# Half of a decoder layer's output product by seven products in the first layer too, its steps dealt out among the other parts

## The chip, the cores and the metric

The kernel runs on one core of one Trainium2 chip. The metric is the time of one execution in device microseconds (us); three runs of the kernel before give 1916.87 us as their median (1916.32 to 1916.96). Engines are named as the profile names them: PE (matmuls), PEld (PE's weight loads), DVE, ACT, POOL, SP.

## The reference

Two decoder layers on 256 tokens (two tiles of 128) of width 2048. Cut to what matters here:

```
for l in range(DEPTH):
    h = rms_norm(x, norm1_g[l])
    z = h @ w_in[l]
    z_sgu = gelu(z[..., :2048])
    out_a = chunked_sgu(z_sgu, sgu_norm_g[l], sgu_w[l], sgu_b[l])
    out_b = swa_sink_attention(q, k, v, ...)          # the other columns of z
    mixed = concatenate([rms_norm(out_a, out_norm_a[l]), rms_norm(out_b, out_norm_b[l])])
    x = x + mixed @ w_out[l]
    h2 = rms_norm(x, norm2_g[l])
    x = x + (silu(h2 @ w_gate[l]) * (h2 @ w_up[l])) @ w_down[l]
```

The place of the change is `mixed @ w_out[l]` for the first layer: a 256 x 2048 by 2048 x 2048 product. The first 1024 rows of `w_out` meet `out_a` (the gated half, "a"), the other 1024 meet `out_b` (attention, "b"). The two normalisations are applied behind the product, as a factor for each token.

## The kernel before, in words

**One unit of product.** Weights come as tiles `raw` of 128 x 1024 (512 KB) over SP's queue into eight buffers. `split2` makes two parts of each in a reduced form of float32: ACT writes `wh` (L118, five buffers), DVE subtracts and writes `wl` (L119, four buffers). `mm3` then runs three matmuls of 128 x 512 for each of 128 rows and each token tile: wh with the high part of the activation (L154), wl with the high part (L155), wh with the low part (L156). A `unit` is 12 such matmuls into two accumulators, one for each token tile.

**Order.** Nothing runs by itself: the program is written as a stream of units, `tick()` adds one to a clock for each unit (a half for a half unit), and small steps (attention, normalisation, transposes) are booked with `later(delay, step)` and put into the program when the clock is due. The tables at the head (`UNIT_AT`, `END_AT`, `PARTS`) are such bookings, a first entry for the first layer and a second for the second. The build then sets the final order on each engine, so that a row may stand some rows from where the program has it.

**The stage.** Behind the q, k, v and gate products stands the product of the two u blocks (`u_gated`), and then the output product in parts: `a0` is column block 0 (512 columns) from the a half, `b2` is column block 2 from the b half. Each part is four units; `PARTS` is their order, one name for a unit. In between come six attention units (`attend`, each with scores `ps_s` L617, a softmax on DVE and ACT, transposes of the probabilities `ps_p` L654 and the product with the values `ps_v` L666), booked by `UNIT_AT`. Four `attend_end` steps, booked by `END_AT`, transpose attention's output `ob` (L227, `ps_t`) and make the activations of the b parts with L217 on ACT and L218 on DVE. `to_T` in `u_gated` transposes the gated u into `aT` for the a parts.

**Banks.** Matmul results go to eight banks: five of the pool `pa` (accumulators), two of `pd`, one of `pm`. `small_ps` hands the small tiles (`ps_s`, `ps_p`, `ps_v`, `ps_t`) round four homes: `pm`, `pd`, `pd`, `pa`. While `few` is set the fourth is left out.

**The second layer already does it the other way.** There `S_OUT` is true: column blocks 2 and 3 of the a half are one product of 2 x 2 blocks by `seven_low`, in 14 half units of six matmuls, each an entry `s` of `PARTS`, in place of eight units. `seven_low` needs the activations also in summed form: `combine_a` makes, beside the usual pair, four sums (L279, L282, L285 on DVE) and splits them into `ext` (L291 on ACT, L292 on DVE). The weights are summed on DVE (L433, L434), and two more sums are made by transfers of POOL's queue that add to what lies in the buffer (`ys` L435, `ss` L440). The products are held in three accumulators `l0`, `l1`, `l2` of `pa`.

Of the kernel before, what the change touches and what calls it, by code (L numbers as in the profile page):

```python
# [46 lines left out]
STD_UNITS = 8 * NFF + 16 * len(GU_BLOCKS)  # L47
TAIL = 16
WARM = 12
UNIT_AT = ((8, 11, 14, 17, 20, 24), (8, 11, 14, 17, 21, 25))  # L50
KV_NORM = (31, 0)
KV_T = (8, 6)
V_NORM = ((12, 2), (0, 0))
# [7 lines left out]
Q_T = (((4, 6), (6, 9)), ((4, 6), (4, 7)))  # L61
SPATIAL_AT = (((8, 10), (9, 11)), ((6, 9), (7, 10)))
U_AT = (((5, 8), (2, 4)), ((3, 7), (2, 3)))
END_AT = (((22, 26), (30, 32)), ((22, 27), (31, 33)))
S_OUT = (False, True)
EXT_A_WAIT = 0.5
FF_FIRST = 5
EXT_AT = (6.5, 8, 11, 13, 16, 18, 21.5, 24)
MASK_AFTER = ((5, 5), (4, 4))
GATE_LOAD = ((24, 29), (5, 15))  # L70
PARTS = (
    "a0 a0 a1 a1 a0 a0 a1 a1 a2 a2 a2 a2 a3 a3 a3 a3 b0 b0 b1 b1 b0 b0 b1 b1 b2 b2 b2 b2 b3 b3 b3 b3",
    "a0 a0 s a0 s a0 a1 a1 s a1 s a1 s b0 s b0 s b0 s b0 s b1 s b1 s b1 s b1 s s b2 b2 b2 b2 b3 b3 b3 b3",
)

# [12 lines left out]
def trunk(ctx, tc, x, xt, w_in, w_q, w_out, w_oa, w_gate, w_up, w_down, sgu_w, sgu_g, consts,  # L88
# [39 lines left out]
    def later(delay, fn):  # L128
        pending.append((clock[0] + delay, next(serial), fn))
# [71 lines left out]
    def small(shape, name):  # L201
        return sp.tile(shape, F32, tag=name, name=name)
# [20 lines left out]
    def transpose_pair(blocks, ps=None):  # L223
        ps = small_ps([P, 2, SEQ], "ps_t") if ps is None else ps
        for j in range(2):
            for t in range(NTOK):
                nc.tensor.transpose(  # L227
                    ps[:, j, t * P : (t + 1) * P], blocks[t][:, j * P : (j + 1) * P], ident
                )
        return ps  # L230
# [5 lines left out]
    def finish_rms(ss, width):  # L236
        tot = small([P, NTOK], "tot")
        nc.vector.tensor_reduce(tot, ss, AX.X, ALU.add)
        r = inv_rms(tot, NTOK, width)
        return [r[:, t : t + 1] for t in range(NTOK)]  # L240
# [64 lines left out]
    def combine_a(ps, lay, col, ext):  # L305
        ge = tp.tile([P, 2, NB], F32, tag="hT", name="ge")
        g = ge[:, 0].rearrange("p (j c) -> p j c", j=2)
        for j in range(2):
            nc.scalar.activation(
                g[:, j, :], ps[:, j, :], AF.Copy, scale=cst[:, lay, col + j : col + j + 1]  # L310
            )
        pair = tp.tile([P, 2, 2, SEQ], F32R, tag="aT", name="aT")
        nc.scalar.copy(pair[:, 0], g)
        nc.vector.tensor_tensor(pair[:, 1], g, f(pair[:, 0]), ALU.subtract)
        extend(g, tp, "hT", ext, EXT_A_WAIT, ge[:, 1].rearrange("p (n c) -> p n c", n=4))
        return pair
# [194 lines left out]
    for lay in range(L):  # L511
# [169 lines left out]
        def attend_end(gp, r, lay=lay, ob=ob, ssb=ssb, pairs_b=pairs_b):  # L681
            if r == 0:
                for t in range(NTOK):
                    sum_sq(ssb[:, t, gp : gp + 1], ob[gp, t])
            g = 2 * gp + r
            ps = transpose_pair([ob[gp, t][:, r * 2 * P : (r + 1) * 2 * P] for t in range(NTOK)])
            pairs_b[g] = split_gain(ps, lay, C_GB + 2 * g, "aT")
# [61 lines left out]
        def u_gated(b, acc, lay=lay, layer=layer, gate=gate, ssa=ssa, pairs_a=pairs_a, ext_a=ext_a):  # L749
# [17 lines left out]
            def to_T(c):  # L767
                ps = transpose_pair([us[t][:, 2 * c * P : (2 * c + 2) * P] for t in range(NTOK)])
                if S_OUT[lay]:
                    pairs_a.append(combine_a(ps, lay, C_GA + 4 * b + 2 * c, ext_a))  # L770
# [50 lines left out]
        for i, (gp, t, i0, n) in enumerate(units):  # L821
            at = UNIT_AT[lay][i]
            later(at, lambda gp=gp, t=t, i0=i0, n=n, attend=attend: attend(gp, t, i0, n))
# [3 lines left out]
        for gp in range(2):  # L827
            for r in range(2):
                later(END_AT[lay][gp][r], lambda gp=gp, r=r, attend_end=attend_end: attend_end(gp, r))
        rstds = {}  # L830

        def finish_mixed(kind, ss, lay=lay, rstds=rstds):
            rstds[kind] = finish_rms(ss, SW)
            if kind == "a" and S_OUT[lay]:
                na = small([P, NTOK], "na")

                def negate():
                    for t in range(NTOK):
                        nc.vector.tensor_scalar(
                            na[:, t : t + 1], rstds["a"][t], -1.0, None, ALU.mult  # L840
                        )

                later(3, negate)
                rstds["na"] = [na[:, t : t + 1] for t in range(NTOK)]

        later(END_AT[lay][1][0] + 1, lambda ssb=ssb, finish_mixed=finish_mixed: finish_mixed("b", ssb))
        if lay > 0:
# [342 lines left out]
```

## Time and profile before

| | |
|---|---|
| median of three runs | 1916.87 us (1916.32 to 1916.96) |
| the profiled execution's own time | 1915.77 us |
| its span | 1914.0 us |
| instructions | 25417 |
| moved by transfers | 456.84 MB, mean 239 GB/s |

The profile is of one execution, and durations are read from it. Its span is 1.77 us shorter than that execution's own time, which holds what lies around the span. Matmuls overlap in the records: one of 128 x 512 is shown with 0.39 us, while the next starts some 0.23 us behind it; what counts is the distance between starts.

### The profile page before, as it was taken

How to read it: one execution, taken by the hardware profiler on the slowest of the kernel's cores; microseconds unless marked ns; L12 is line 12 of the kernel's file. 1: busy time of each engine (PE TensorE's matmuls, PEld its weight loads, DVE VectorE, ACT ScalarE, POOL GpSimd, SP SyncE). 2: the span in 40 equal slices, each digit the busy share in tenths (PEclk: the TensorE clock that was granted, in tenths of full speed). 3: DMA queues.
4: the chain of work that ended last, by engine and by line, in shares of the span. 5: the costliest groups of instructions: out<-in, count | busy, mean ns of one | idle time of the engine just before them, and what ended most of it. 6: DMA issues, size and time to landing. Idle time of an engine off the chain costs nothing.

```text
span 1914.0 us, 25417 instructions
## 1 busy us (share of the span) xinstructions
PE 1907.2 (100%) x8776; PEld 1569.2 (82%) x8776; DVE 1709.5 (89%) x1853; ACT 1353.1 (71%) x1814; POOL 182.5 (10%) x176
## 2 busy tenths in 40 slices
PE   9999999999999999999999999999999999999999
PEld 7888888888888888888888888888888888888887
DVE  7987689999999999999796778899999999999993
ACT  8668577677767776777777577766877677766774
POOL 0231001000100001000012201000000100010000
PEclk9999999999999999999999999999999999999999
DMA  9974448888877897888577537697789778888783
GB/s 355 262 284 154 135 160 239 255 247 276 267 237 245 271 292 226 249 255 288 187 216 263 182 120 232 191 271 231 242 269 295 229 247 266 277 243 252 251 273 112
DMA packets 127425, 456.84 MB, mean 239 GB/s; under 512 B 14144, under 2 KB 14528, under 8 KB 127296
## 3 DMA queue, kind: packets, MB, share of 16 engines
q1 hardware_dynamic: 105264, 376.44, 53.5%
q0 software_dynamic: 21312, 77.60, 22.2%
q8 instruction: 68, 1.11, 0.2%
q10 hardware_dynamic: 720, 1.18, 0.2%
q14 instruction: 61, 0.50, 0.1%
HBM read 453.07 MB, written 2.10 MB: 238 GB/s over the span
## 4 chain that ended last, share of the span: by engine, by line
PE 97%; issue 1%; DVE 1%; ACT 0%; POOL 0%; DMA 0%; SPq 0%; DVEq 0%; ACTq 0%; POOLq 0%
PE m L155 15%; PE m L154 15%; PE m L156 15%; PE dacc L154 11%; PE dacc L155 11%; PE dacc L156 11%; PE acc L154 5%; PE acc L155 5%; PE acc L156 5%; PE ps_v L666 1%; PE ps_f L227 1%; PE ps_s L617 1%; PE ps_n L227 1%; PE ps_p L654 0%; PE ps_t L227 0%
## 5 line engine op out<-in xcount | busy, mean ns | idle before, releaser
L118 ACT CAST wh<-raw 128x1024 fp32r<-128x1024 f32 (+1 forms) x794 | 815.3, 1050 | 396.6 <-DVE raw L350 168.7
L119 DVE TENSOR_TENSOR wl<-raw,wh 128x1024 fp32r<-128x1024 f32 (+1 forms) x794 | 944.7, 1217 | 99.2 <-ACT wh L118 25.9
L154 PE MATMUL m<-wh,ext 128*128 128x512 f32 x704 | 276.7, 393 | 0.0
L155 PE MATMUL m<-wl,ext 128*128 128x512 f32 x704 | 274.9, 391 | 0.0
L156 PE MATMUL m<-wh,ext 128*128 128x512 f32 x704 | 274.4, 390 | 0.0
L155 PE MATMUL dacc<-wl,aT 128*128 128x512 f32 x624 | 243.4, 390 | 0.0
L154 PE MATMUL dacc<-wh,aT 128*128 128x512 f32 x624 | 243.2, 391 | 0.0
L156 PE MATMUL dacc<-wh,aT 128*128 128x512 f32 x624 | 243.0, 389 | 0.0
L119 DVE TENSOR_TENSOR wl<-t,wh 128x1024 fp32r<-128x1024 f32 x176 | 213.0, 1219 | 12.7 <-issue 5.2
L118 ACT CAST wh<-t 128x1024 fp32r<-128x1024 f32 x176 | 184.5, 1051 | 37.6 <-DVE t L351 14.1
L154 PE MATMUL m<-wh,hT 128*128 128x512 f32 x528 | 206.4, 391 | 0.0
L155 PE MATMUL m<-wl,hT 128*128 128x512 f32 x528 | 205.7, 390 | 0.0
L156 PE MATMUL m<-wh,hT 128*128 128x512 f32 x528 | 205.5, 389 | 0.0
L155 PEld LDWEIGHTS m<-wl,ext 128*128 128x128 f32 x704 | 132.3, 188 | 29.0 <-DVE wl L119 2.1
L154 PEld LDWEIGHTS m<-wh,ext 128*128 128x128 f32 x704 | 132.2, 188 | 27.5 <-ACT wh L118 0.8
L156 PEld LDWEIGHTS m<-wh,ext 128*128 128x128 f32 x704 | 132.1, 188 | 27.5
L154 PEld LDWEIGHTS dacc<-wh,aT 128*128 128x128 f32 x624 | 117.2, 188 | 25.2 <-ACT wh L118 0.8
L155 PEld LDWEIGHTS dacc<-wl,aT 128*128 128x128 f32 x624 | 117.2, 188 | 24.8 <-DVE wl L119 0.6
L156 PEld LDWEIGHTS dacc<-wh,aT 128*128 128x128 f32 x624 | 117.2, 188 | 24.3
L154 PE MATMUL acc<-wh,aT 128*128 128x512 f32 x304 | 121.8, 402 | 0.0
L359 POOL DMA_DIRECT2D t<-in_w_gate_dram x80 | 69.3, 866 | 524.7 <-DVE wl L119 393.1
L156 PE MATMUL acc<-wh,aT 128*128 128x512 f32 x304 | 119.1, 392 | 0.0
(190 smaller groups left out, 2841.9 us busy)
## 6 DMA issues: line engine op xcount, KB each, us to landing
raw<-in_w_gate_dram SPq DMA_DIRECT2D x176, 512.0 KB, 5.9
raw<-in_w_up_dram SPq DMA_DIRECT2D x176, 512.0 KB, 6.0
raw<-in_w_down_dram SPq DMA_DIRECT2D x176, 512.0 KB, 5.9
t<-in_w_gate_dram POOLq DMA_DIRECT2D x80, 512.0 KB, 7.6
raw<-in_w_in_dram SPq DMA_DIRECT2D x76, 512.0 KB, 5.6
raw<-in_w_out_dram SPq DMA_DIRECT2D x56, 512.0 KB, 3.4
raw<-in_w_up_dram POOLq DMA_DIRECT2D x40, 512.0 KB, 6.1
raw<-in_w_q_dram SPq DMA_DIRECT2D x32, 512.0 KB, 5.2
```

The lines of the kernel that those rows point to most:

```text
L118: nc.scalar.copy(wh[:, j : j + step, :], src)
L119: nc.vector.tensor_tensor(wl[:, j : j + step, :], src, f(wh[:, j : j + step, :]), ALU.subtract)
L154: nc.tensor.matmul(acc, ah, wh, start=first, stop=False, skip_group_check=again)
L155: nc.tensor.matmul(acc, ah, wl, start=False, stop=False, skip_group_check=again)
L156: nc.tensor.matmul(acc, al, wh, start=False, stop=last, skip_group_check=again)
L227: nc.tensor.transpose(ps[:, j, t * P : (t + 1) * P], blocks[t][:, j * P : (j + 1) * P], ident)
L359: anchor[0] = nc.gpsimd.dma_start(t2, src(1, 0, i), accum_op=ALU.add)
L617: nc.tensor.matmul(ps[r][:, i, :], qT[gp][rows, i0 + i, t * P : (t + 1) * P], kT[rows, gp, :nk], start=True, stop=True,)
L666: nc.tensor.matmul(pv[:, r, i], pt[:, (r * n + i) * (t + 1) + b, :], zkv[b][:, cols], start=b == 0, stop=b == t,)
```

## The change

Three tables of the first layer change. `S_OUT` becomes true for it, so that parts a2 and a3 (eight units) go and 14 half units `s` come. `PARTS` deals these out among a0, a1, b0 and b1, so the b parts begin five units of the clock sooner. `UNIT_AT` and `END_AT` move the attention steps of the first layer forward by half a tick to five ticks.

```
-UNIT_AT = ((8, 11, 14, 17, 20, 24), (8, 11, 14, 17, 21, 25))
+UNIT_AT = ((7.5, 10, 12.5, 15.5, 18, 20.5), (8, 11, 14, 17, 21, 25))
...
-END_AT = (((22, 26), (30, 32)), ((22, 27), (31, 33)))
-S_OUT = (False, True)
+END_AT = (((21, 23.5), (25.9, 27)), ((22, 27), (31, 33)))
+S_OUT = (True, True)
...
 PARTS = (
-    "a0 a0 a1 a1 a0 a0 a1 a1 a2 a2 a2 a2 a3 a3 a3 a3 b0 b0 b1 b1 b0 b0 b1 b1 b2 b2 b2 b2 b3 b3 b3 b3",
+    "a0 a0 a1 a1 s a0 a0 s a1 s a1 s s s b0 s b0 s b0 s b0 s b1 s b1 s b1 s b1 s b2 b2 b2 b2 b3 b3 b3 b3",
```

In the final order of each engine the two programs are the same up to the second u block and again from block b2 on, tile numbers apart. PE has 96 matmuls of 128 x 512 fewer for a2 and a3, and 84 for the 14 half units: 12 fewer. The stretches of small tiles between such matmuls number 23 where they were 25. DVE gets 6 splits more (L119), 4 sums of weights (L433, L434), 4 times L279, L282, L285, L292 and L314 in place of 8 times L218, and 2 of L865 fewer at each accumulator for 4 of L872 and 2 sums of results. ACT has two loads of its function table fewer.

On PE, at the first place, the scores of the fourth attention unit (`ps_s`) stand ahead of two groups of transposes. Before, all matmuls of one bank come first and then those of the other, and a unit of part a0 follows:

```order
L654 MATMUL ps_p_1814<-ident_103,s_1682 128x128 x4
L654 MATMUL ps_p_1820<-ident_103,s_1682 128x128 x4
L617 MATMUL ps_s0_1827<-kT_123,qT1_125 128x128 x4
L617 MATMUL ps_s1_1828<-kT_123,qT1_125 128x128 x4
L154 MATMUL acc0_1616<-wh_1849,aT_1790 128x512
```

Now they alternate between the two banks, and the transposes of the last gated u (`ps_t_1841`) follow a matmul later:

```order
L617 MATMUL ps_s0_1808<-kT_123,qT1_125 128x128
L617 MATMUL ps_s1_1809<-kT_123,qT1_125 128x128
L617 MATMUL ps_s0_1808<-kT_123,qT1_125 128x128
L617 MATMUL ps_s1_1809<-kT_123,qT1_125 128x128
L654 MATMUL ps_p_1829<-ident_103,s_1647 128x128 x4
L654 MATMUL ps_p_1835<-ident_103,s_1647 128x128 x4
L154 MATMUL acc0_1627<-wh_1878,aT_1729 128x512
L227 MATMUL ps_t_1841<-ident_103,u_1622 128x128
L227 MATMUL ps_t_1841<-ident_103,u_1624 128x128
```

What moved: the scores have the next transposes close behind, where they had a whole unit of 12. Four accumulators (a0 and a1) are open here, so `ps_s0_1808` has the fifth bank of `pa`, and `ps_t_1841` is booked on the same one.

On PE, at the second place, the first `attend_end` (`ps_t` from `ob`) and the transposes of the next probabilities. Before:

```order
L227 MATMUL ps_t_2003<-ident_103,ob_1783 128x128
L666 MATMUL ps_v_2015<-zkv_340,pt_1924 128x64 x8
L154 MATMUL acc0_1956<-wh_2028,aT_1712 128x512
L155 MATMUL acc0_1956<-wl_2029,aT_1712 128x512
L156 MATMUL acc0_1956<-wh_2028,aT_1712 128x512
```

behind which stand nine matmuls more of the same unit, and then `ps_p`. Now:

```order
L227 MATMUL ps_t_2065<-ident_103,ob_1780 128x128
L666 MATMUL ps_v_2077<-zkv_340,pt_1974 128x64 x8
L654 MATMUL ps_p_2089<-ident_103,s_1921 128x128 x4
L154 MATMUL l1_2013<-wh_2108,ext_1760 128x512
L155 MATMUL l1_2013<-wl_2109,ext_1760 128x512
L156 MATMUL l1_2013<-wh_2108,ext_1760 128x512
L154 MATMUL l1_2013<-wh_2108,ext_1873 128x512
L654 MATMUL ps_p_2095<-ident_103,s_1921 128x128 x4
L155 MATMUL l1_2013<-wl_2109,ext_1873 128x512
```

What moved: between `ps_t_2065` and `ps_p_2095`, which take the same bank of `pd` one after the other, there are four large matmuls. Three homes are in turn here, four before.

On DVE, at the same place, the drains of that bank are the two L218 on `aT_2070`. Before, the rows around them (`aT_2008`) are:

```order
L119 TENSOR_TENSOR wl_2099<-raw_2096,wh_2098 128x1024
L659 TENSOR_TENSOR rden_1950<-den_1949,es_1948 128x4
L660 RECIPROCAL rden_1950<-rden_1950 128x4
L119 TENSOR_TENSOR wl_2135<-raw_2132,wh_2134 128x1024
L218 SCALAR_TENSOR_TENSOR aT_2008<-ps_t_2003,cst_82,aT_2008 128x256
L673 TENSOR_TENSOR ob_2024<-ps_v_2015,rden_1843 128x512
L218 SCALAR_TENSOR_TENSOR aT_2008<-ps_t_2003,cst_82,aT_2008 128x256
```

Now:

```order
L119 TENSOR_TENSOR wl_2123<-ys_1858,wh_2122 128x1024
L622 SCALAR_TENSOR_TENSOR s_2025<-ps_s0_2026,bias_1664 128x512
L622 SCALAR_TENSOR_TENSOR s_2025<-ps_s1_2027,bias_1666 128x512
L119 TENSOR_TENSOR wl_2133<-ys_1959,wh_2132 128x1024
L631 TENSOR_REDUCE m_2034<-s_2025 128x4
L218 SCALAR_TENSOR_TENSOR aT_2070<-ps_t_2065,cst_82,aT_2070 128x256
L632 SCALAR_TENSOR_TENSOR nm_2035<-m_2034,nsink_608 128x4
L673 TENSOR_TENSOR ob_2086<-ps_v_2077,rden_1824 128x512
L633 TENSOR_TENSOR es_2036<-nm_2035,nsink_608 128x4
L865 SCALAR_TENSOR_TENSOR xres_108<-acc0_1740,ir2_1786,xres_108 128x512
L218 SCALAR_TENSOR_TENSOR aT_2070<-ps_t_2065,cst_82,aT_2070 128x256
```

What moved: the scores and the maximum of the sixth attention unit, a split of a summed weight `ys` and an update of the residual now stand ahead of the second drain.

## Prediction

> **What bounds the kernel now.** I read the page first: busy times, then the chain of work that ended last.
>
> ```profile
> PE 1907.2 (100%) x8776; PEld 1569.2 (82%) x8776; DVE 1709.5 (89%) x1853; ACT 1353.1 (71%) x1814; POOL 182.5 (10%) x176
> PE 97%; issue 1%; DVE 1%; ACT 0%; POOL 0%; DMA 0%; SPq 0%; DVEq 0%; ACTq 0%; POOLq 0%
> ```
>
> PE is the bound from end to end, and the chain is PE's own order. So a matmul taken away is time won, one for one, and whatever else the change does costs nothing until PE has to wait for it. Whether PE waits today at the place of the change is read from the windows of the first layer's attention and output stage (start and end, length, then busy us and instructions of PE, PEld, DVE, ACT, POOL, the clock, the DMA share, GB/s), and from two of the second layer, where the same product already runs by halves.
>
> ```profile
> 160.00:180.00 20.00, 19.95 (x118) 16.25 (x117) 13.77 (x25) 19.55 (x42) 0.89 (x1) 1.00 0.30 100
> 180.00:200.00 20.00, 20.00 (x119) 17.27 (x118) 14.47 (x25) 15.39 (x42) 0.73 (x1) 1.00 0.48 159
> 200.00:220.00 20.00, 20.00 (x112) 16.23 (x111) 14.64 (x22) 10.00 (x20) 0.00 (x0) 1.00 0.42 137
> sum 160.00, PE 159.94 PEld 133.02 DVE 117.88 ACT 110.91 POOL 8.78; mean PE 19.99 PEld 16.63 DVE 14.74 ACT 13.86 POOL 1.10
> 1140.00:1160.00 20.00, 20.00 (x115) 17.14 (x114) 17.54 (x34) 15.73 (x34) 2.50 (x3) 1.00 0.54 161
> 1160.00:1180.00 20.00, 20.00 (x92) 16.21 (x91) 17.14 (x21) 13.09 (x18) 3.17 (x3) 1.00 0.88 224
> ```
>
> PE does not wait (159.94 of 160 us from 140 to 300 us); the clock is full, and DVE has a quarter of the time free (117.88 of 160). The second layer runs its halves without a wait of PE, with DVE at 17.5 of 20; but there all six attention units are through, or nearly so, when the halves begin. In the first layer the two now fall together, with ACT at 19.55 of 20 in one window already. That decides the case.
>
> **What PE has less of.** The distance between starts, from the timeline of PE:
>
> ```profile
> 163.11 0.39 PE L155 MATMUL acc<-wl,hT 128*128 128x512 f32 x1
> ...
> 165.41 0.39 PE L156 MATMUL acc<-wh,hT 128*128 128x512 f32 x1
> 165.65 0.60 PE L227 MATMUL ps_t<-ident,u 128*128 128x128 f32 x4
> 166.08 0.60 PE L227 MATMUL ps_t<-ident,c 128*128 128x128 f32 x4
> ...
> 187.22 1.03 PE L654 MATMUL ps_p<-ident,s 128*128 128x128 f32 x8
> 188.19 1.95 PE L617 MATMUL ps_s<-kT,qT 64*128 64x128 f32 x16
> 190.07 0.50 PE L154 MATMUL acc<-wh,aT 128*128 128x512 f32 x1
> ...
> 150.52 1.16 PE L617 MATMUL ps_s<-kT,qT 64*128 64x128 f32 x16
> 151.61 0.50 PE L154 MATMUL acc<-wh,hT 128*128 128x512 f32 x1
> ...
> 201.19 1.13 PE L617 MATMUL ps_s<-kT,qT 64*128 64x256 f32 x8
> 202.25 0.50 PE L154 MATMUL acc<-wh,aT 128*128 128x512 f32 x1
> 202.59 0.40 PE L155 MATMUL acc<-wl,aT 128*128 128x512 f32 x1
> ```
>
> 1. Ten steps from 163.11 to 165.41 make 0.230 us for a large matmul. Twelve fewer: 12 x 0.230 = 2.76 us.
> 2. The scores of the fourth attention unit, all of one bank first, took 188.19 to 190.07, 1.88 us. Sixteen of the same size whose order alternates between two banks took 150.52 to 151.61, 1.09 us. In the change the fourth unit's alternate too: 0.79 us less.
> 3. Back from small tiles the first large matmul takes 0.34 us (202.25 to 202.59), 0.11 more than the others. Two such returns fewer: 0.2 us.
>
> Together 3.75 us. None of it can be lost on PE itself; it can only be given back by waits.
>
> **What the other engines have more of.** The forms, from the groups kept apart by shape:
>
> ```profile
> L119 DVE TENSOR_TENSOR wl<-raw,wh 128x1024 fp32r<-128x1024 f32 x790 | 942.1, 1220 | 98.9 <-ACT wh L118 25.7 <-PE acc L155 22.7 <-issue 19.0
> L434 DVE TENSOR_TENSOR ss<-raw 128x1024 f32<-128x1024 f32 x2 | 2.4, 1214 | 0.0
> L865 DVE SCALAR_TENSOR_TENSOR xres<-acc,ir,xres 128x512 f32<-128x512 f32 x28 | 19.9, 746 | 7.2 <-PE acc L156 7.2
> L622 DVE SCALAR_TENSOR_TENSOR s<-ps_s,bias 128x512 f32<-128x512 f32 x24 | 15.5, 684 | 3.6 <-PE ps_s L617 3.5
> L218 DVE SCALAR_TENSOR_TENSOR aT<-ps_t,cst,aT 128x256 fp32r<-128x256 f32 x24 | 11.5, 481 | 6.6 <-ACT aT L217 6.3
> L631 DVE TENSOR_REDUCE m<-s 128x4 f32<-128x1024 f32 x8 | 9.8, 1220 | 0.2
> L279 DVE TENSOR_TENSOR ge<-ge 128x256 f32<-128x256 f32 x4 | 1.7, 419 | 0.8 <-ACT ge L309 0.8
> L314 DVE TENSOR_TENSOR aT<-ge,aT 128x512 fp32r<-128x512 f32 x4 | 2.7, 683 | 0.0
> L118 ACT CAST wh<-raw 128x1024 fp32r<-128x1024 f32 x790 | 813.0, 1052 | 396.6 <-DVE raw L350 168.7 <-PE dacc L156 96.1 <-PE acc L156 57.6
> L753 ACT ACT_TABLE_LOAD x4 | 5.1, 1283 | 0.1
> 180.76 2.35 DVE L119 TENSOR_TENSOR wl<-raw,wh 128x1024 fp32r<-128x1024 f32 x2
> 157.36 0.40 ACT L638 ACTIVATE s<-s,nm 128x128 f32<-128x128 f32 x1 [4.38 <-DVE nm L632]
> 179.11 1.62 POOL L210 TENSOR_TENSOR ir<-ms,mhalf 128x2 f32<-128x2 f32 x1 [25.83 <-DVE ms L208]
> ```
>
> DVE gets some 19 us more (10 of 1.22 for splits and sums of weights, four times about 2.3 for the summed activations, less eight L218 of 0.48, and little else), ACT about 9. Two L119 in a row take 2.35, so a seam saves up to 0.08. Over the stage DVE goes from 74% to about 87% and would still be hidden; six transfers more are hidden by a DMA share of 0.3 to 0.5. The cost is local. I followed the queues in the new order and found three places where PE can wait.
>
> (a) The transposes of the last gated u (`ps_t_1841`). They need the bank that the fourth unit's scores leave, hence its first L622. From the end of the second u block PE has 49 large matmuls (11.3), 16 transposes of 0.108 (1.7), 16 `ps_p` (0.97 for eight, 187.22 to 188.19: 1.9), 32 `ps_v` (about 3.4), two sets of scores (1.06 and 1.09) and its returns (0.5): 21.0 us. On the other side ACT first ends two softmaxes: from 157.36 there are twelve exponentials, two casts, a pair of copies, the summed activations and a table load, 11.5 us in all, so it comes to the gelu at 168.9, about 3.4 behind the block's end (165.4). Then 3.3 on ACT (two gelu, two L309, L589, L313), 1.25 on DVE, and DVE's rows from the third unit's scores to the fourth's: five L119 (5.9), three L622 (2.0), L631 (1.2) and some 4 of smaller ones, 13.1, with a wait of 1.8 for POOL's L210 ahead of the negated factor L839 and 0.5 for a cast. Together 23.4, that is 2.4 late. I take 2.1, since PE is held a little before. Ends: 0, if ACT comes to the gelu as soon as the block ends (today it does), and 3.5, without the seams.
>
> (b) `ps_p_2095`, which needs the bank of `ps_t_2065`, free behind the second L218 on `aT_2070`. It is reckoned from the same L622 that (a) waits for, so it adds to (a). DVE: the other L622 and the maximum (1.85), then up to that L218 six L119 and four sums (10 of 1.22), four L622, two L631, three L865, two L673, the fifth activation's sums (2.3), two L218 and eight short ones: 25.4 by the means, 23.7 with seams; in all 25.5. PE: 69 large (15.9), 32 `ps_v` (3.4), two sets of scores (2.1), 12 `ps_p` (1.45), 8 transposes (0.9), returns (0.6): 24.3. DVE has more than PE here, and `ps_p_2095` is **1.2 us** late. Ends: 0, with the second layer's windows as witness, and 3.2, without seams.
>
> (c) Third activation of the b parts (`aT_2262`): on ACT a cast (`wh_2367`) stands between its two halves and waits for a buffer. I take 0.2; ends 0 and one cast, 1.05.
>
> Waits: 2.1 + 1.2 + 0.2 = 3.5 us, between 0 and 7.75. Net -3.75 + 3.5 = -0.25. Against the profiled execution (1915.77, span 1914.0) that is 1915.5; the median of the runs lies 1.1 higher, so **1916.6**.
>
> **Two rules weighed.** In (a) and (b) PE waits for a bank, and the second layer's windows above, with the same three homes, show no wait. The Trainium skill, Perfetto Trace Analysis, Optimizing Tensor Performance, would have matmul groups rotate through different PSUM banks so that draining one overlaps the next group's matmuls; that speaks against fewer homes. By the rule (a) and (b) stand; by the windows alone the sum would be 1913.3.
>
> ```profile
> L435 POOL DMA_DIRECT2D ys<-in_w_oa_dram x2 | 1.8, 893 | 8.2 <-ACT wh L118 5.3 <-DVE rden L660 2.9
> ys<-in_w_oa_dram POOLq DMA_DIRECT2D x2, 512.0 KB, 5.4
> ss<-in_w_oa_dram POOLq DMA_DIRECT2D x2, 512.0 KB, 8.7
> ```
>
> POOL's adding transfers were issued in 0.893 us beside a DVE that was busy 17 of 20, and `ys` landed in 5.4. The Trainium skill, SBUF — State Buffer, two separate sides, warns that a transfer issued by GpSimd can sit without descriptors while DVE holds the port they share. By that rule they would land later, which is the slower rival below; the rows show no sign of it in 0.893 us.
>
> **The rivals.**
>
> - *Forecast: the win is eaten by waits at a few places* (waits of 1.5 to 5 us, 1914.6 to 1918.1). Chance 0.52.
> - *No wait to speak of* (below 1.5): seams and slack do a little better than I reckon, as in the second layer. For it: no row of before shows PE waiting. Against: 25.5 of DVE against 24.3 of PE. Time 1913.1 to 1914.5, 1913.3 at its middle. Chance 0.26, of which 0.07 beyond -0.2%.
> - *Slower*: the second `ys` is late. It is issued behind the second L433, and by my reckoning lands (5.4) just as ACT wants to cast it. Behind that cast on ACT stand L217, two copies and the sixth unit's exponentials, and behind these DVE's second L218 and PE. Each us beyond 5.6 is a us of PE. At the 8.7 of `ss` the wait grows by 3.1, time 1919.7; from 9.7 on the kernel is slower by over 0.2%, and at 11 it takes 1922. For it: 8.7 was seen. Against: both `ys` took 5.4. Chance 0.14.
> - *Waits of 5 to 7.5 at several places*, still within 0.2%: 0.08.
>
> **How the numbers follow.** 0.2% is 3.8 us, about what a measurement of this kernel can tell from no change. Faster by more: 0.07, the edge of the no-wait case. Slower by more: 0.14. Within: 0.79. The range goes from the no-wait case (1913.1) to the sum of the upper ends, 1916.87 - 3.75 + 7.75 = 1920.9, drawn in a little on both sides: 1913.2 to 1920.6.
>
> **What would show it.** PE's 12 matmuls and the scores at 1.09: certain, to be read in the page's count (8764) and the timeline. For (a) a gap on PE ahead of four L227 from u, released by DVE's L622; for (b) one ahead of four L654 between matmuls of `l`, released by DVE's L218; for the slower rival, ACT idle ahead of L118 on `ys`, released by a transfer. From block b2 on nothing should differ but the offset. I am wrong if PE waits at another place for longer than 2 us, or if the later stages are moved by more than the offset.

## The result, and the profile after

| | before | changed |
|---|---|---|
| median | 1916.84 us (22 runs) | 1913.90 us (22 runs) |
| the profiled execution's own time | 1915.77 us | 1913.70 us |
| its span | 1914.0 us | 1912.0 us |

The ratio is 0.9984, 95% interval 0.9978 to 0.9991: 2.9 us less, between 1.7 and 4.2. The forecast was 1916.6 with 1913.2 to 1920.6 as its range; what came is the rival "no wait to speak of" (1913.1 to 1914.5), which had 0.26.

The busy times and the chain that ended last, of the changed kernel:

```profile
PE 1903.6 (100%) x8764; PEld 1565.2 (82%) x8764; DVE 1725.1 (90%) x1879; ACT 1361.0 (71%) x1829; POOL 183.4 (10%) x180
PE 95%; ACT 2%; issue 1%; DVE 1%; DMA 1%; POOL 0%; SPq 0%; DVEq 0%; ACTq 0%; POOLq 0%
```

PE has its 12 matmuls less, DVE 15.6 us more (1709.5 before; some 19 were reckoned). The chain is still PE's, but ACT now has 2% of it, where it had none: from 157.3 to 184.0 us the chain runs on ACT, nearly without a break. The windows of the stage show what PE loses there:

```profile
160.00:180.00 20.00, 20.00 (x119) 16.66 (x118) 16.41 (x31) 19.94 (x48) 0.30 (x1) 1.00 0.38 126
180.00:200.00 20.00, 19.34 (x122) 15.81 (x122) 18.43 (x33) 16.64 (x45) 1.33 (x2) 1.00 0.46 133
sum 160.00, PE 159.34 PEld 131.38 DVE 135.03 ACT 120.24 POOL 11.41; mean PE 19.92 PEld 16.42 DVE 16.88 ACT 15.03 POOL 1.43
```

DVE is at 135.0 of 160 us, 84%, near the 87% reckoned. PE lacks 0.66 us in all, and all of it between 180 and 200. The timeline of PE there, then rows of DVE and of ACT from the same stretch:

```profile
183.93 1.16 PE L617 MATMUL ps_s<-kT,qT 64*128 64x128 f32 x16
185.03 1.09 PE L654 MATMUL ps_p<-ident,s 128*128 128x128 f32 x8
185.87 0.48 PE L154 MATMUL acc<-wh,aT 128*128 128x512 f32 x1
187.02 0.66 PE L227 MATMUL ps_t<-ident,u 128*128 128x128 f32 x4 [0.66 <-DVE s L622]
```

```profile
180.45 0.21 DVE L839 TENSOR_SCALAR na<-ir 128x1 f32<-128x1 f32 x2 [0.84 <-POOL ir L210]
184.00 2.36 DVE L119 TENSOR_TENSOR wl<-raw,wh 128x1024 fp32r<-128x1024 f32 x2 [0.56 <-ACT wh L118]
186.28 1.28 DVE L622 SCALAR_TENSOR_TENSOR s<-ps_s,bias 128x512 f32<-128x512 f32 x2
```

```profile
168.57 0.69 ACT L753 ACTIVATE u<-acc,ir 128x512 f32<-128x512 f32 x1
182.92 2.94 ACT L118 CAST wh<-raw 128x1024 fp32r<-128x1024 f32 x3
```

This is the wait (a) of the prediction, at its place and with its releaser: four L227 from u stand behind DVE's L622. From 185.87 to 187.02 are 1.15 us, 0.23 of them the matmul itself, so PE loses 0.9, where 2.1 was reckoned. Scores of the fourth unit: 183.93 to 185.03, 1.10 us, as reckoned.

The second place, on PE, DVE and ACT:

```profile
211.14 0.64 PE L654 MATMUL ps_p<-ident,s 128*128 128x128 f32 x4
```

```profile
211.47 0.49 DVE L218 SCALAR_TENSOR_TENSOR aT<-ps_t,cst,aT 128x256 fp32r<-128x256 f32 x1
```

```profile
210.48 0.59 ACT L655 COPY pt<-ps_p 128x512 f32<-128x512 f32 x1 [1.76 <-PE ps_p L654]
```

Wait (b) did not come. And it could not have: `ps_p_2095` starts at 211.14, 0.33 us ahead of the second L218 for which it was to wait. It does not stand in that bank.

The slower rival's transfer, on POOL, and the cast that waits for it, on ACT:

```profile
200.66 0.87 POOL L435 DMA_DIRECT2D ys<-in_w_oa_dram  x1 [6.51 <-ACT pt L655]
```

```profile
206.07 1.05 ACT L118 CAST wh<-ys 128x1024 fp32r<-128x1024 f32 x1 [1.59 <-DMA ys<-in_w_oa_dram]
```

The second `ys` lands 5.4 us behind its issue (200.66 to 206.07), and ACT waits 1.6 us for it, as the rival had it. PE does not wait: it is busy for 20.00 of the 20 us from 200 to 220.

Last, one matmul behind the stage, of block b2, in the two kernels; from here on they are the same:

```profile
263.23 0.48 PE L154 MATMUL acc<-wh,aT 128*128 128x512 f32 x1
```

```profile
260.55 0.48 PE L154 MATMUL acc<-wh,aT 128*128 128x512 f32 x1
```

The changed kernel is 2.68 us ahead here. It was 0.08 ahead at 150 us already, before the two programs differ, so 2.6 us are won. To the end the offset moves between 2.3 and 2.7 us: the prediction's "From block b2 on nothing should differ but the offset" held. With the 0.9 of wait (a) PE's own saving is 3.5, where 3.75 was reckoned.

### The profile page after: what moved, and what is told of

Its sections match the earlier page's. It is cut to its first block, busy times and chain, and to the rows that moved or that the text cites. A ratio compares the mean times of both kernels' runs of the same rounds, so it can differ in the third digit from the quotient of the medians.

```text
span 1912.0 us, 25453 instructions
## 1 busy us (share of the span) xinstructions
PE 1903.6 (100%) x8764; PEld 1565.2 (82%) x8764; DVE 1725.1 (90%) x1879; ACT 1361.0 (71%) x1829; POOL 183.4 (10%) x180
## 4 chain that ended last, share of the span: by engine, by line
PE 95%; ACT 2%; issue 1%; DVE 1%; DMA 1%; POOL 0%; SPq 0%; DVEq 0%; ACTq 0%; POOLq 0%
PE m L155 15%; PE m L154 15%; PE m L156 15%; PE dacc L154 11%; PE dacc L155 11%; PE dacc L156 11%; PE acc L154 4%; PE acc L155 4%; PE acc L156 4%; PE ps_f L227 1%; PE ps_v L666 1%; PE l L154 1%; PE l L155 1%; PE l L156 1%; PE ps_n L227 1%
## 5 line engine op out<-in xcount | busy, mean ns | idle before, releaser
L119 DVE TENSOR_TENSOR wl<-raw,wh 128x1024 fp32r<-128x1024 f32 (+1 forms) x794 | 945.1, 1219 | 92.4 <-ACT wh L118 26.5
L155 PE MATMUL m<-wl,ext 128*128 128x512 f32 x704 | 274.9, 391 | 0.0
L155 PE MATMUL dacc<-wl,aT 128*128 128x512 f32 x624 | 243.4, 390 | 0.0
L119 DVE TENSOR_TENSOR wl<-t,wh 128x1024 fp32r<-128x1024 f32 x176 | 213.6, 1223 | 12.9 <-issue 5.4
L155 PE MATMUL m<-wl,hT 128*128 128x512 f32 x528 | 205.7, 390 | 0.0
L155 PEld LDWEIGHTS m<-wl,ext 128*128 128x128 f32 x704 | 132.3, 188 | 28.9 <-DVE wl L119 2.0
L155 PEld LDWEIGHTS dacc<-wl,aT 128*128 128x128 f32 x624 | 117.2, 188 | 24.8 <-DVE wl L119 0.6
L156 PEld LDWEIGHTS dacc<-wh,aT 128*128 128x128 f32 x624 | 117.2, 188 | 24.3
L156 PEld LDWEIGHTS m<-wh,hT 128*128 128x128 f32 x528 | 99.1, 188 | 20.7
L155 PEld LDWEIGHTS m<-wl,hT 128*128 128x128 f32 x528 | 99.2, 188 | 20.3
```

Source lines behind the costliest of these rows:

```text
L119: nc.vector.tensor_tensor(wl[:, j : j + step, :], src, f(wh[:, j : j + step, :]), ALU.subtract)
L155: nc.tensor.matmul(acc, ah, wl, start=False, stop=False, skip_group_check=again)
L156: nc.tensor.matmul(acc, al, wh, start=False, stop=last, skip_group_check=again)
```

## The experiments

Each was run beside the kernel before on the same chip; compare the ratios, since the chips differ by some tenths of a us. The changed kernel has 0.9984. Where an execution differs from another already ahead of the stage (up to 1.4 us by 50 us, in the first loads), that is taken off below.

| | median | before, same chip | ratio, 95% interval |
|---|---|---|---|
| unit_at_only | 1916.87 | 1916.79 | 0.9998, 0.9989 to 1.0007 |
| s_contig | 1920.69 | 1916.79 | 1.0022, 1.0012 to 1.0032 |
| negate_later | 1913.82 | 1916.79 | 0.9983, 0.9974 to 0.9992 |
| u_at_5_5 | 1919.81 | 1916.79 | 1.0012, 1.0003 to 1.0021 |
| u_at_3 | 1914.27 | 1917.57 | 0.9984, 0.9976 to 0.9993 |
| squares_64 | 1914.28, one run | 1917.57 | none |
| by_bank | 1914.97 | 1917.57 | 0.9986, 0.9977 to 0.9996 |
| squares_later | 1912.98 | 1916.93 | 0.9981, 0.9972 to 0.9990 |
| two_pd | 1914.14 | 1916.93 | 0.9985, 0.9976 to 0.9994 |
| ys_late | 1923.13 | 1917.57 | 1.0030, 1.0017 to 1.0042 |

**The two halves of the change**

The attention units alone, on the kernel before:

```
-UNIT_AT = ((8, 11, 14, 17, 20, 24), ...
+UNIT_AT = ((7.5, 10, 12.5, 15.5, 18, 20.5), ...
```

> The kernel before with the change's earlier attention units alone (UNIT_AT), no half units in the first layer. Theory: the fourth unit's scores alternate between two banks here as well and take 1.1 instead of 1.9 us, nothing else on PE gets shorter, and DVE, without the half units, drains the bank in time: 0.6 to 0.9 us less than before, 1915.9 to 1916.3 us, PE's gap ahead of the last u transposes below 0.3 us. Rival (the earlier attention brings most of the gain): 1914.5 us or less. Rival (the earlier attention costs, and the half units bring all): 1916.9 us or more.

No change in the time, so neither the 0.8 us expected nor more. By the rows the stage costs 0.2 us more than before (this execution is 0.86 us late ahead of it and 1.04 behind it). The scores did get shorter (186.24 to 187.33), and a wait that I did not expect took it back: PE first, then ACT, of this kernel.

```profile
172.91 0.66 PE L654 MATMUL ps_p<-ident,s 128*128 128x128 f32 x4 [1.04 <-DVE aT L218]
...
186.24 1.16 PE L617 MATMUL ps_s<-kT,qT 64*128 64x128 f32 x16
```

```profile
171.60 0.49 ACT L217 ACTIVATE aT<-ps_t,cst 128x256 fp32r<-128x256 f32 x1
```

The transposes wait for a bank that L217 and L218 drain, and these L217 stand on ACT behind exponentials, a table load (from 168.22, 1.28 us) and two gelu. Attention moved up fills ACT, and PE waits for it, here too.

The half units alone, all in a row, attention where it was:

```
-    "a0 a0 a1 a1 s a0 a0 s a1 s a1 s s s b0 s b0 s b0 s b0 s b1 s b1 s b1 s b1 s b2 ...
+    "a0 a0 a1 a1 a0 a0 a1 a1 s s s s s s s s s s s s s s b0 b0 b1 b1 b0 b0 b1 b1 b2 ...
```

> The first layer's a2 and a3 by the 14 half units as in the change, but all 14 in a row behind a0 and a1, and the attention steps where they were before the change. Theory (the gain is PE's own time, and dealing the half units out among full units is what keeps it, because DVE has more to do for a half unit than PE): PE has the same 12 matmuls fewer (-2.8 us), but in the row of half units DVE has 14 splits and 4 sums of 1.22 us (22 us) and some 14 us of attention beside 84 matmuls and small tiles (26.5 us on PE), with four wl buffers of lead (5 us), so PE waits 3 to 8 us there: 1917 to 1922 us, with gaps ahead of L155 released by DVE's L119. Rival (only the number of matmuls counts, the places do not matter): 1913.5 to 1914.2 us and no gap over 0.5 us.

The size came, the cause was another. On POOL, ACT and PE, then the window behind:

```profile
204.98 0.86 POOL L440 DMA_DIRECT2D ss<-in_w_oa_dram  x1 [4.06 <-DVE wl L119]
207.24 0.86 POOL L435 DMA_DIRECT2D ys<-in_w_oa_dram  x1 [1.39 <-DVE nm L632]
```

```profile
214.96 1.04 ACT L118 CAST wh<-ys 128x1024 fp32r<-128x1024 f32 x1 [3.50 <-DMA ys<-in_w_oa_dram]
```

```profile
216.06 0.50 PE L154 MATMUL l<-wh,ext 128*128 128x512 f32 x1 [1.58 <-ACT wh L118]
217.31 0.80 PE L155 MATMUL l<-wl,ext 128*128 128x512 f32 x1 [0.76 <-DVE wl L119]
217.91 0.63 PE L156 MATMUL l<-wh,ext 128*128 128x512 f32 x1
218.33 0.63 PE L154 MATMUL l<-wh,ext 128*128 128x512 f32 x1
```

```profile
218.00:220.00 2.00, 2.00 (x7) 1.35 (x5) 0.00 (x0) 0.15 (x1) 0.00 (x0) 0.50 0.03 6
```

DVE, which I had for the bound, is idle for most of that time (0.00 in this window). What is late is the second `ys`: it was issued behind an `ss` and lands 7.7 us behind its issue, with half units only, and no full one, between its issue and its use. Behind the two waits the granted clock is 0.50, and matmuls stand 0.42 apart (217.91 to 218.33) where 0.23 is usual. The two waits (1.75 and 1.03 us by the distance between starts) and the slow matmuls behind them (some 1.6) make 4.4 of the 7.1 us that this kernel is behind the changed one; the rest is not split up here. So the larger part of what dealing out the half units wins is that the late `ys` stays hidden.

**Wait (a)**

The change's small negations, which wait for POOL, put behind the L622 on DVE:

```
+                    with tc.issue_after(scored[0].ins):   # scored[0]: the last L622
                         for t in range(NTOK):
                             nc.vector.tensor_scalar(na[:, t : t + 1], ...
```

> The changed kernel with the two small L839 (the negated factor, which waits for POOL's L210) held back behind the fourth unit's L622 on DVE. It takes 0.84 us of DVE's idle time and 0.2 us of its work out ahead of the L622 on which PE's 0.9 us wait hangs. Theory after the result (ACT is last there: DVE then waits for the casts of the two wh that stand ahead, ACT having no idle time since 157 us): the wait stays at 0.8 to 0.95 us and the time at 1913.9 us (1913.6 to 1914.2). Rival (the prediction's own chain: DVE with its wait for POOL is last): the wait goes to 0.1 us or less, 1913.0 us.

On DVE and PE (lines are one higher with the edit):

```profile
185.42 2.36 DVE L119 TENSOR_TENSOR wl<-raw,wh 128x1024 fp32r<-128x1024 f32 x2 [0.83 <-ACT wh L118]
187.70 1.28 DVE L623 SCALAR_TENSOR_TENSOR s<-ps_s,bias 128x512 f32<-128x512 f32 x2
```

```profile
186.44 1.09 PE L655 MATMUL ps_p<-ident,s 128*128 128x128 f32 x8
...
188.43 0.66 PE L228 MATMUL ps_t<-ident,u 128*128 128x128 f32 x4 [0.67 <-DVE s L623]
```

The wait for POOL is gone, and DVE waits 0.83 for ACT's cast instead of 0.56. The L622 starts 1.26 behind the end of the scores (186.44 to 187.70), in the changed kernel 1.25 (185.03 to 186.28). Without the wait for POOL the L622 comes no earlier: ACT is last here, where the prediction's sum has DVE's rows with that wait. L210 takes 0.72 us in both executions.

Less work on ACT there, with most of a sum left out:

```
-                    sum_sq(ssa[:, t, b : b + 1], u)
+                    sum_sq(ssa[:, t, b : b + 1], u if lay or b == 0 else u[:, :64])
```

> The changed kernel with the sums of squares of the second u block (L234 on ACT) taken over 64 of the 512 columns only, which leaves most of that sum out: ACT has some 0.9 us less ahead of the casts that stand before the fourth unit's L622. The build also puts the u transposes one large matmul earlier. Theory (ACT is last in the chain to that L622): DVE's idle time ahead of the L119 there (0.56 us) goes, the first L622 ends 0.4 to 0.6 us earlier against the scores, and the PE wait, counted with the matmul that no longer stands ahead of it, gets 0.3 to 0.6 us shorter: 1913.3 to 1913.6 us. Rival (DVE itself is last, through its wait for POOL): the L622 ends where it did.

On PE, with ACT between its two waits:

```profile
186.67 0.66 PE L227 MATMUL ps_t<-ident,u 128*128 128x128 f32 x4 [0.53 <-DVE s L622]
...
211.50 0.66 PE L654 MATMUL ps_p<-ident,s 128*128 128x128 f32 x4 [0.33 <-ACT pt L655]
```

```profile
208.52 1.05 ACT L118 CAST wh<-ys 128x1024 fp32r<-128x1024 f32 x1 [3.69 <-DMA ys<-in_w_oa_dram]
```

The first L622 starts at 185.93 instead of 186.28, 0.35 us earlier, though ACT comes 0.7 us earlier to the table load behind the squares (176.50 for 177.22). PE gains nothing by it: the matmul that stood ahead of the transposes now stands behind them, and PE comes to the next L155 at 187.40 (187.43 in the changed kernel), so the 0.3 to 0.6 us expected did not come. What holds the L622 now is the rival's chain: in this execution POOL's L210 takes 1.63 us (0.72 in the changed kernel), DVE's L839 and the sums L279 to L285 wait for it, and ACT's L291, ahead of the casts, waits 0.26 us for L285 (it starts at 181.47). ACT is last in the changed kernel, then, but POOL's chain stands close behind it. Further on, the first `ss` went out ahead of the second `ys`, which landed 7.6 us behind its issue (200.91), and PE lost 0.5 at `ps_p`.

Two that move the waiting transposes instead:

```
-U_AT = (((5, 8), (2, 4)), ...
+U_AT = (((5, 8), (2, 5.5)), ...        and in the other kernel (2, 3)
```

> The changed kernel with the last transposes of u booked one and a half ticks later (U_AT 4 to 5.5), so that they no longer take the bank of the fourth unit's scores: nothing waits for that L622. Theory (the one wait seen on PE is worth its length and nothing takes it back): no gap over 0.3 us in the stage, 0.9 us less than the changed kernel, 1913.0 us (1912.7 to 1913.4). Rival (what is won there is lost again where weights have little lead, 0.8 to 1.5 us near 202 and 220 us, or where the summed activations now come late): gaps of 0.5 us or more at other places, 1913.9 us or more.

> The changed kernel with the last transposes of u one tick earlier (U_AT 4 to 3): they now stand a whole unit of 12 large matmuls ahead of the fourth unit's scores, take the fifth bank of the accumulators there, and nothing close behind the scores needs a bank that the first L622 drains. The steps behind keep their order on PE, and the second ys keeps its place. Theory (the 0.9 us wait is worth its length where nothing else is moved; the kernel with U_AT 5.5 lost because its second ys was issued 2.7 us later): no gap over 0.3 us in the stage, 1913.0 us (1912.6 to 1913.4). Rival (ACT, which has no idle time there, now does two scaled copies and two splits more ahead of the weights' casts, and the wait comes back at the probabilities' transposes or at a weight): a gap of 0.5 us or more, 1913.9 us or more.

PE of the first, then of the second:

```profile
187.11 0.50 PE L154 MATMUL l<-wh,aT 128*128 128x512 f32 x1 [0.66 <-DVE s L622]
```

```profile
189.04 0.50 PE L154 MATMUL l<-wh,aT 128*128 128x512 f32 x1 [0.73 <-ACT pt L655]
```

In both, the accumulator `l0` now waits 0.9 us for a bank (1.14 us from the matmul ahead of it, 0.23 of them that one's own): for 5.5 the bank that L622 drains, for 3, by the releaser, one that ACT's copies L655 drain. Moving the one who waits moves the wait. For 3 the rival held; for 5.5 a gap of over 0.5 us came, as in its rival, but the 4 us behind it were in neither expectation. The kernel with 5.5 lost 7 us in all, most of it at the second `ys`, which now stands behind the first `ss` (202.28) on POOL; POOL, ACT and PE:

```profile
203.40 0.86 POOL L435 DMA_DIRECT2D ys<-in_w_oa_dram  x1 [0.26 <-DVE raw L433]
```

```profile
212.89 1.04 ACT L118 CAST wh<-ys 128x1024 fp32r<-128x1024 f32 x1 [5.48 <-DMA ys<-in_w_oa_dram]
```

```profile
215.87 1.12 PE L654 MATMUL ps_p<-ident,s 128*128 128x128 f32 x4 [3.96 <-ACT pt L655]
```

The scores by banks, in both layers, to price their alternation:

```
-            for i in range(n):
-                for r in range(2):
+            for r in range(2):
+                for i in range(n):
```

> The changed kernel with the scores of every attention unit written bank by bank (all matmuls of the lower 64 rows, then all of the upper 64) in both layers, in place of alternating. Theory (matmuls of 64 rows run in pairs when their row halves alternate, which gave the change 0.8 us at the fourth unit): each of the four sets of 16 takes 1.9 instead of 1.1 us, +3.2 us, and each of the eight sets of 8 (64x256) 0.1 to 0.8 us more: 1917.9 to 1923.5 us. Rival (the 0.8 us had another cause, such as the weight loads or the bank of the neighbours): 1913.7 to 1914.3 us.

PE and DVE at the fourth unit:

```profile
184.29 1.71 PE L617 MATMUL ps_s<-kT,qT 64*128 64x128 f32 x16
185.93 1.09 PE L654 MATMUL ps_p<-ident,s 128*128 128x128 f32 x8
186.94 0.66 PE L227 MATMUL ps_t<-ident,u 128*128 128x128 f32 x4
```

```profile
186.20 1.28 DVE L622 SCALAR_TENSOR_TENSOR s<-ps_s,bias 128x512 f32<-128x512 f32 x2
```

Neither expected time came. The build alternated some of them again, so sets of 16 took 1.64 us to the next instruction and sets of 8 stayed at 1.07. In the first layer two sets are 0.55 longer each, and yet PE's later rows stand only 0.1 to 0.25 us later than in the changed kernel: the L622 begins at 186.20 as ever, PE comes later, and wait (a) is gone. So the price exists and the time hardly shows it. As long as wait (a) stands, what PE saves ahead of that L622 is worth nothing, since ACT sets when PE goes on.

What the others point to: ACT's squares put back to where it is idle, nothing left out.

```
+SQ_AT = 3.1
...
+                    with tc.issue_after(copied[0].ins):   # copied[0]: the last L655
+                        for t, u in enumerate(us):
+                            sum_sq(ssa[:, t, b : b + 1], u)
...
-                later(3, negate)
+                later(3 if lay else 0.5, negate)
...
-        later(3, lambda ssa=ssa, finish_mixed=finish_mixed: finish_mixed("a", ssa))
+        later(3 if lay else SQ_AT + 1.5, lambda ssa=ssa, finish_mixed=finish_mixed: finish_mixed("a", ssa))
```

> The changed kernel with the two sums of squares of the second u block (L234, 1.35 us of ACT) held back behind the copies of the third unit's probabilities, and what hangs on them (L210 on POOL, the L839) booked later; nothing is left out, and the second ys still goes ahead of the adding ss. Theory (the 0.9 us wait is ACT's backlog since 157 us, so it goes only where ACT loses work ahead of the weights' casts; there ACT then has idle time to take the squares back): the first L622 ends within 0.3 us of the end of the scores, no gap over 0.3 us on PE in the stage, 0.7 to 1.0 us less than the changed kernel, 1912.9 to 1913.3 us on a chip where that one takes 1913.9. Rival (what is won there is taken back by the residual updates, which now wait for POOL's L210, or by a weight with little lead): a gap of 0.4 us or more at another place and 1913.9 us.

ACT and DVE (lines are two higher), and the window:

```profile
184.13 1.05 ACT L119 CAST wh<-raw 128x1024 fp32r<-128x1024 f32 x1 [0.35 <-PE acc L158]
```

```profile
185.22 1.29 DVE L624 SCALAR_TENSOR_TENSOR s<-ps_s,bias 128x512 f32<-128x512 f32 x2
```

```profile
180.00:200.00 20.00, 20.00 (x126) 16.45 (x126) 18.76 (x38) 16.55 (x46) 1.64 (x2) 1.00 0.47 132
```

ACT is through early enough to wait for a buffer itself, the L622 follows the scores by 0.1 us, and PE is busy for 20.00 of 20. Behind the stage PE's rows stand 0.9 us ahead of the changed kernel's, the size expected. The edit takes both chains out of the way, ACT's squares and, with them, L210 and the L839 that waits for it (L210 starts at 193.54 here): it shows that the wait goes when both do, not that ACT's part alone would be enough. The medians agree with that (3.95 us under before, against 2.94), though the two intervals overlap.

**Wait (b)**

The two banks of `pd` as pools of one, so that the turn alone decides:

```
-    pd = ctx.enter_context(tc.tile_pool(name="pd", bufs=2, space=PSUM))
+    pd = ctx.enter_context(tc.tile_pool(name="pd", bufs=1, space=PSUM))
...
-        homes = ((pm, "sm"), (pd, "dacc"), (pd, "dacc"), (pa, "acc"))
+        homes = ((pm, "sm"), (pd, "dacc0"), (pd, "dacc1"), (pa, "acc"))
```

> The changed kernel with the two banks of pd as two pools of one, so that the third small tile after ps_t_2065 must take its bank, as the prediction reckoned, where the changed kernel gives ps_p_2095 the bank of ps_p_2089. The build then puts ps_p_2095 behind ten large matmuls in place of four. Theory (that wait was missing because banks and order are chosen together, by what is free first, and not by the turn): PE comes to ps_p_2095 some 0.5 us behind the second L218, no gap over 0.4 us there, 1913.6 to 1914.3 us. Rival (the prediction's term of 1.2 us stands as soon as the bank is shared): a gap of 0.8 to 1.6 us ahead of ps_p_2095, released by DVE's L218, 1914.8 us or more.

DVE and PE:

```profile
211.54 0.48 DVE L221 SCALAR_TENSOR_TENSOR aT<-ps_t,cst,aT 128x256 fp32r<-128x256 f32 x1
```

```profile
212.57 0.60 PE L657 MATMUL ps_p<-ident,s 128*128 128x128 f32 x4
```

Now `ps_p_2095` does follow the drain, 0.55 us behind its end (212.02), and PE has filled the time with ten matmuls of `l1` and `l2`. The bank is as I had reckoned it, and there is still no wait.

**The slower rival**

The second `ys` issued behind the first adding `ss`, nothing else (the second layer has the same edit):

```
-            anchor[0] = nc.gpsimd.dma_start(y[i], src(1, 1, i), accum_op=ALU.add)
+            if i == 0:
+                anchor[0] = nc.gpsimd.dma_start(y[i], src(1, 1, i), accum_op=ALU.add)
...
+            if i == 0:
+                with tc.issue_after(anchor[0].ins):   # behind the adding ss
+                    anchor[0] = nc.gpsimd.dma_start(y[1], src(1, 1, 1), accum_op=ALU.add)
```

> The changed kernel with one transfer held back: the second adding ys is issued behind the first adding ss on POOL, so some 4 us later than in the changed kernel (204.7 instead of 200.7 us); everything else is as the build then orders it. Theory (the prediction's slower rival, seen by accident in two kernels: ACT stands at the cast of ys, and the copies, the exponentials and the next transposes stand behind it): ys lands between 210 and 214 us, ACT is idle ahead of its L118 until then, PE waits 2 to 6 us ahead of ps_p L654 or of L155, and behind that wait the granted clock falls to 0.5 for some 5 us, which costs another 1 to 2 us: 1917 to 1922 us. Rival (PE has 5.3 us of lead on this weight, and the build reorders around it): 1913.7 to 1914.3 us and no gap over 0.5 us.

POOL, ACT, PE and two windows (lines differ with the edit):

```profile
202.76 0.86 POOL L441 DMA_DIRECT2D ss<-in_w_oa_dram  x1 [7.40 <-DVE es L637]
203.30 1.20 POOL L444 DMA_DIRECT2D ys<-in_w_oa_dram  x1
```

```profile
214.31 1.04 ACT L118 CAST wh<-ys 128x1024 fp32r<-128x1024 f32 x1 [8.63 <-DMA ys<-in_w_oa_dram]
```

```profile
217.29 1.12 PE L658 MATMUL ps_p<-ident,s 128*128 128x128 f32 x4 [4.58 <-ACT pt L659]
```

```profile
212.00:214.00 2.00, 0.71 (x4) 0.23 (x2) 0.00 (x0) 0.00 (x0) 0.00 (x0) 1.00 1.04 242
...
218.00:220.00 2.00, 2.00 (x7) 1.61 (x7) 1.50 (x4) 1.78 (x7) 0.00 (x0) 0.50 0.00 0
```

The rival's mechanism, whole: late `ys`, ACT idle, PE without a bank for `ps_p`, and then a clock of 0.50. In the first layer this costs 6.0 us, 4.7 of wait and 1.3 of slow matmuls, and 2.4 more in the second. Issue to cast was 11.0 us: the DMA engines were at their full share (1.04), and `ss` was ahead of it on POOL's queue. How much of the delay is the queue's order, and how much the weights that SP loads at the same time, is not separated here.

## Why the prediction was right, and where not

- **The bound and PE's saving.** Right: 3.5 us by the rows, reckoned 3.75. "None of it can be lost on PE itself" held, but not all of it was to be had: by_bank shows that what PE saves ahead of the fourth unit's L622 goes into wait (a). The 0.79 for the scores and the 0.9 of the wait are in good part one item, booked twice with opposite signs.
- **Wait (a), 2.1 reckoned, 0.9 measured.** The place, the bank and the releaser were right. The terms: PE's side 20.9 (165.20 to the end of the matmul at 185.87, for 21.0). ACT's first gelu at 168.57, 3.4 behind the block, as reckoned. DVE's side 21.8 instead of 23.4: the third unit's L622 came 7.7 us behind the block instead of 8.0, DVE's rows from there took 12.6 instead of 13.1, and the wait ahead of L839 was 0.84 instead of 1.8, since POOL's L210 took 0.72 us this time and 1.62 before. That last, the largest part, is luck: nothing in the change makes L210 shorter, and the prediction had taken its 1.62. With L210 at 0.72 the step that puts "a wait of 1.8 for POOL's L210" into the chain fails: negate_later shows that ACT's casts are last then. But not by much: in the changed kernel the sums on DVE end at 181.64, 0.2 us ahead of ACT's L291, and in squares_64, with L210 at 1.63, they are what ACT waits for. An estimate from these rows: with L210 at 1.62 in the changed kernel, wait (a) would be some 0.7 us longer. squares_later shows that the wait goes when both chains are relieved.
- **Wait (b), 1.2 reckoned, none.** The step that failed is "`ps_p_2095`, which needs the bank of `ps_t_2065`". It was reckoned from the turn of three homes, and what stands ahead of the prediction, that the two "take the same bank of `pd` one after the other", is wrong in the same way. In the built program `ps_p_2095` has the bank of `ps_p_2089`, drained by ACT's L655 at 211.07, and so the one that came free first. The sums of that step were good (the second L218 ends at 211.96, 25.0 us behind the end of the first L622, for 25.5; PE comes at 211.14, 24.2 behind it, for 24.3). Even where the bank is shared, two_pd shows, the build chooses another order and no wait comes.
- **Wait (c), 0.2 reckoned, none seen.** No gap above 0.15 us stands on PE there.
- **The slower rival, 0.14.** It did not come, as `ys` landed in the 5.4 us of the profile before. Its price is shown: 1 us of PE for each us. Its threshold was too low. The cast came 2.45, 6.8 and 8.2 us later than in the changed kernel in squares_64, u_at_5_5 and ys_late, and PE lost 0.5, 4.1 and 4.7 there; with PE itself 0.6 and 1.4 us later in the last two, each leaves 2.0 to 2.1 us of slack, so PE waits from a landing of some 7.4 us on, not 5.6. What I missed is the clock's part, 1.3 us more in ys_late and 2.4 in u_at_5_5. The rule that I weighed, from the Trainium skill, SBUF — State Buffer, two separate sides, is not seen at work in these landings: the DMA engines, which by that rule would lie idle, were at a share of 1.02 to 1.05 in every window of ys_late from 206 to 214, with DVE busy until 210 and idle behind.
- **The rule on banks** (the Trainium skill, Perfetto Trace Analysis, Optimizing Tensor Performance): the trace agrees at (a), where one bank goes straight from a drain to the next group; at (b) the build does the rotating.

The forecast case, a win eaten by waits, did not come: of 3.5 us of waits 0.9 came. The time lies within the range only because the range reached down to the case without waits, 0.7 us below what was measured. I gave the likeliest place to a sum of three waits, each reckoned from one chain with all else held in order. Of these, the build had taken (b) apart by giving the tile another bank, (a) came at less than half its size, and why (c) did not come no run shows. And 0.2% was too coarse as what a measurement can tell from no change: 22 runs each leave an interval of 0.9978 to 0.9991.

## What to carry to other kernels

A saving on the bound engine counts only as far as the next place where that engine waits for another: find that place first, and take the savings ahead of it off the wait, not beside it. Which bank or buffer a tile has, and what an instruction waits for, is read from the built program and not from the rule by which the code hands them out. When an engine without idle time sets a wait, moving the one who waits moves the wait; taking work from that engine, to where it is idle later, ends it.

## What the runs showed of the hardware

- The granted clock of PE fell to 0.50 behind 4.0 and 4.6 us of idle time (u_at_5_5, ys_late), and also behind two waits of 1.6 and 0.8 us close together (s_contig); behind one of 0.9 it stayed at 1.00. Matmuls then stand 0.43 us apart for some 3 to 6 us. The Trainium skill, TensorE: Matmul & The Clock Gate, HAM oscillation, tells of this for waits above some 3.4 us; s_contig shows it with 2.3 us in all.
- The second adding transfer `ys` of 512 KB landed between 5.4 and 11.0 us behind its issue: 5.4 in the changed kernel, 7.6 to 11.0 in the four kernels where an adding `ss` stood ahead of it on POOL's queue (squares_64, s_contig, u_at_5_5, ys_late). In the changed kernel the `ss`, issued behind `ys`, took 10.0 (median of two).
- POOL's L210 on 128x2 took from 0.7 to 1.8 us: in the profile before 1.62 at 179.1 us and 0.72 at 1148.2, and at the first of these places 0.72 in the changed kernel, 1.63 in squares_64 and 1.82 in s_contig. No run shows why.
- Matmuls of 64 rows whose row halves alternate start in pairs (0.01 us apart in the changed kernel's scores at 183.93): sixteen of them took 1.1 us alternating, 1.64 partly so, 1.88 bank by bank.
